# A trunk of two mixers and two FFNs: deferred conversions behind the norms, and a scan traced in two steps

## The chip, the cores and the metric

The kernel runs on one core of one Trainium2 chip. The metric is the device time of one execution in microseconds (us). A kernel has several runs, and the median is quoted.

## The reference

For one sequence of 512 tokens with 1024 features, two layers are computed. Layer 0 has a Mamba-2 (SSD) mixer, layer 1 an RG-LRU mixer; a causal ConvFFN follows each. Every part is wrapped in two RMSNorms:

```python
for i in range(DEPTH):
    h = rmsnorm(x, norm_mix_pre[i])
    m = ssd_mixer(h, ...) if i % 2 == 0 else rglru_mixer(h, ...)
    x = x + rmsnorm(m, norm_mix_post[i])
    h = rmsnorm(x, norm_ffn_pre[i])
    f = conv_ffn(h, ...)
    x = x + rmsnorm(f, norm_ffn_post[i])
```

`ssd_mixer` projects `h` to z (2048), to x, B and C (3072, through a causal convolution of 4 taps and silu) and to dt (32 heads). It scans in 4 chunks of 128 tokens for each of 4 groups of heads, gates by silu(z), norms by group, and projects by `w_out`. `rglru_mixer` projects to two branches of 1280, runs a gated linear recurrence, and projects back with a bias `b_out`. `conv_ffn` projects up to 8192, convolves with 3 taps, takes gelu(g) * v and projects down from 4096. All is float32.

## The kernel before

Four phases follow one another: the SSD mixer (`ssd`), an FFN (`ffn`), the RG-LRU mixer (`lru`), an FFN. The residual `xr` stays on chip as 4 tiles of 128 tokens x 1024 features. The input `h` of a phase is held transposed, features on partitions, as two halves `hh` (rounded to fp32r) and `hl` (the rest), so that each float32 product is made of three fp32r matmuls: `up_mm` (L227 to L229), `down_mm` (L251), `pair_mm` (L553). Each weight tile is a DMA of 512 KB on SP into `r` (class `Weight`), a rounding copy on ACT (L209) and a subtraction on DVE (L210). So ACT and DVE work in step with every 24 matmuls or so.

At the end of a phase, `down` (for the SSD mixer the loop at the end of `ssd`) holds back the last 5 (SSD: 4) weight tiles and runs them token tile by token tile, so that tile 0 is finished early. `epilogue(t)` then takes the accumulators of tile t:

- `post_norm`: squares on ACT (L190), the reciprocal root on GpSimd (L162, L163, `rstd`), the product on DVE (L193), and the residual add (L194), on GpSimd but in the last phase
- `pre_norm`: squares (ACT L169), `rstd`, product (DVE L172) into `hb`
- `transpose_h`: eight transposes on PE (L179), then `hh` on ACT (L182) and `hl` on DVE (L183)

The next phase begins with four weight tiles, which `load_ahead` loads and converts (called in the epilogue of tile 0). Their matmuls run first over tiles 0 and 1, then over tiles 2 and 3 (`HALVES`). After them come the loops over the other weights, with convolutions on ACT (L298) and DVE (L300).

The order on each engine isn't the order of the code: a scheduler of the framework places the instructions by its own simulation, and `tc.issue_after(i)` forbids it to place an instruction ahead of i. Each engine then runs its queue in order.

In `ssd`, `conv_tile` makes a projected and convolved tile. `scan_group(g)` runs the four chunks of a group: loads the decays (`cs_d`, L395), makes masked scores (L397, ACT L419 to L425, DVE), transposes (L403, L409), the weighted rows `xdt` and, on GpSimd, `xdd` (L414, which needs `dout`, made by ACT L364), then the products (L430, L432) and the state (L444). `gate(g)` projects z and norms the group by matmuls with ones and the identity (its z tiles, then a rate, then a scale). `late_consts` loads rows of constants (L144), transposes them (L147) and prepares the RG-LRU's constants after the first scan. In `lru`, `biased` adds `b_out` to each accumulator on DVE (L639) and hands the sum to the epilogue.

At the start, x tiles 0 and 1 come as two DMAs each, then the first gain as a broadcast to 128 partitions (`load_gain`, L115), and the first two `pre_norm`s.

Of the kernel before, what the change touches and what calls it, by code (L numbers as in the profile page):

```python
# [13 lines left out]
P = 128  # L14
# [6 lines left out]
NG = 4  # L21
# [54 lines left out]
def tile_trunk(ctx: ExitStack, tc: tile.TileContext, x, norm_mix_pre, norm_mix_post, norm_ffn_pre, norm_ffn_post,  # L76
# [41 lines left out]
    def load_x(t):  # L118
        for i in range(2):
            dma(xr[:, t, cols(i)], x[0, t * P:(t + 1) * P, cols(i)])  # L120

    load_x(0)
    qg = load_gain(norm_mix_pre[0])
    load_x(1)
    for i, a in enumerate((ssd_dt_bias, ssd_a_log)):
        dma(small_tiles["hrow"][i:i + 1, :], a)
    dma(small_tiles["dall"], ssd_d.to_broadcast([P, NH]))
# [4 lines left out]
    G.memset(ones, 1.0)  # L132
    stat_ids = list(range(48))
# [5 lines left out]
    def const_cols(name, parts, banks):  # L139
        n = sum(a.shape[0] for a in parts)  # L140
        rows = S2.get()
        o = 0
        for a in parts:
            dma(rows.ap[o:o + a.shape[0], 0:P], a)  # L144
            o += a.shape[0]
        pt = banks.get()
        T.transpose(pt.ap[:, 0:n], rows.ap[0:n, 0:P], ident[0:n, 0:n])  # L147
        c = small_tiles[name]
        V.tensor_copy(c, pt.ap[:, 0:n])
        rows.free()  # L150
        pt.free()
        return c
# [8 lines left out]
    def rstd(st):  # L161
        G.tensor_scalar(out=st[:, 2:3], in0=st[:, 0:1], scalar1=st[:, 1:2], scalar2=EPS, op0=ALU.add, op1=ALU.add)  # L162
        G.tensor_tensor(out=st[:, 2:3], in0=st[:, 2:3], in1=nhalf[:, 0:1], op=ALU.pow)  # L163
        return st[:, 2:3]

    def pre_norm(t, hb, qg):
        st = small()
        for i in range(2):
            A.activation(hb.ap[:, cols(i)], xr[:, t, cols(i)], AF.Square, scale=1.0 / 32, accum_out=st[:, i:i + 1])  # L169
        r = rstd(st)  # L170
        for i in range(2):
            V.scalar_tensor_tensor(out=hb.ap[:, cols(i)], in0=xr[:, t, cols(i)], scalar=r, in1=qg.ap[:, cols(i)],  # L172
                                   op0=ALU.mult, op1=ALU.mult)
# [13 lines left out]
    def post_norm(t, src, hb, pg, final):  # L187
# [3 lines left out]
        r = rstd(st)  # L191
# [62 lines left out]
    def down(w, nk, get, done, prep, epilogue, gt, last=False):  # L254
        acc = [[PS.get(), PS.get()] for t in range(NT)]
        held = []
        for k in range(nk):
# [5 lines left out]
            ops = (a, wt.wh[:, 0, :], wt.wl[:, 0, :], k == 0, k == nk - 1)  # L263
# [40 lines left out]
    def ssd(h, prep, epilogue):  # L304
# [83 lines left out]
        def scan_group(g, bT, cT):  # L388
            hs = slice(8 * g, 8 * g + 8)
            ent = None  # L390
            for c in range(NT):
# [14 lines left out]
                pt.free()  # L406
                if c < NT - 1:
# [7 lines left out]
                psy = X.get()  # L415
# [5 lines left out]
                V.tensor_tensor(out=scv, in0=scv, in1=cbm.unsqueeze(1).to_broadcast([P, 8, P]), op=ALU.mult)  # L421
                if c > 0:
# [4 lines left out]
                csb.free()  # L427
                for e in range(8):
# [13 lines left out]
                if c < NT - 1:  # L442
# [11 lines left out]
                    ent = nent  # L454
            ent.free()


        def gate(g):
            sq = None
            for m in range(4 * g, 4 * g + 4):  # L460
# [19 lines left out]
            st = small()  # L480
            V.tensor_scalar(out=st, in0=pt.ap[:, 0:NT], scalar1=1.0 / 512, scalar2=EPS, op0=ALU.mult, op1=ALU.add)
            pt.free()
            G.tensor_tensor(out=st, in0=st, in1=nhalf, op=ALU.pow)
            V.tensor_copy(sq.ap.rearrange("p (a b) -> p a b", a=NT), st.unsqueeze(2).to_broadcast([P, NT, P]))
            pt = X.get()
            for t in range(NT):
                T.matmul(pt.ap[:, t * P:(t + 1) * P], sq.ap[:, t * P:(t + 1) * P], ident, start=True, stop=True)
            sq.free()
            for m in range(4 * g, 4 * g + 4):
                ym = y_of(m)  # L490
                V.scalar_tensor_tensor(out=ym, in0=ym, scalar=consts["clru"][:, 100 + m:101 + m], in1=pt.ap, op0=ALU.mult, op1=ALU.mult)
            pt.free()

        for g in range(NG):
            bc = SG.get()
            bT, cT = bc.ap[:, 0:S], bc.ap[:, S:2 * S]
            w = wbc if g == 0 else [up_w(w_in, DI + (16 + g) * P), up_w(w_in, DI + (20 + g) * P)]
            toks = HALVES if g == 0 else [FULL]
            conv_tile(16 + g, w[0], bT, toks)
            conv_tile(20 + g, w[1], cT, toks)  # L500
            for m in range(4 * g, 4 * g + 4):
                conv_tile(m, up_w(w_in, DI + m * P), y_of(m), [FULL])
            if g > 0:
                gate(g - 1)
            scan_group(g, bT, cT)
            bc.free()
            if g == 0:
                late_consts(X)
        gate(NG - 1)
# [46 lines left out]
    def lru(h, prep, epilogue):  # L556
# [10 lines left out]
        for m in range(NL):  # L567
            if m % 4 == 0:
                n = min(4, NL - m)
                wg = Weight([w_[0, m:m + n].rearrange("h i o -> i h o") for w_ in (lru_w_gx, lru_w_ga)], n, n * 256)  # L570
            if m < 4:
                w, pt = first[m], pts[m]
            else:
                w, pt = up_w(w_in, LW + m * P), M.get()
                up_mm(pt, w, h, FULL)
            w.free()

            xb = S2.get()
            conv(xb.ap, pt.ap, 4, lambda q: clru[:, 10 * q + m:10 * q + m + 1], lcor[:, m, 3:4])
            pt.free()  # L580
            V.tensor_tensor(out=xb.ap[:, 0:3], in0=xb.ap[:, 0:3], in1=lcor[:, m, 0:3], op=ALU.add)
            xa = Act(xb.ap, LO)
            pg = [X.get(), X.get()]
            for i in range(2):
                b = 2 * (m % 4) + i
                T.matmul(pg[i].ap, wg.wh[:, b, :], xa.ah, start=True, stop=False)
                T.matmul(pg[i].ap, wg.wh[:, b, :], xa.al, start=False, stop=False)
                T.matmul(pg[i].ap, wg.wl[:, b, :], xa.ah, start=False, stop=True)
            if m % 4 == 3:
                wg.free()  # L590


            bm, thm, am = (s[m // 2].ap[:, cols(m % 2)] for s in (bt, th, at))
            A.activation(bm, pg[0].ap, AF.Sigmoid, bias=clru[:, 70 + m:71 + m])
            A.activation(am, pg[1].ap, AF.Sigmoid, bias=clru[:, 80 + m:81 + m])
            for s in pg:
                s.free()
            V.tensor_tensor(out=bm, in0=bm, in1=xb.ap, op=ALU.mult)
            V.tensor_scalar(out=am, in0=am, scalar1=0.0, scalar2=None, op0=ALU.max)
            last = A.activation(thm, am, AF.Tanh, scale=spl[:, m:m + 1])  # L600
            for s in (xb, xa):
                s.free()
# [31 lines left out]
        bo = load_gain(lru_b_out[0])  # L634

        def biased(t, acc):
            mb = row4()
            for i in range(2):
                V.tensor_tensor(out=mb.ap[:, cols(i)], in0=acc[i].ap, in1=bo.ap[:, cols(i)], op=ALU.add)  # L639
                acc[i].free()  # L640
            epilogue(t, [mb])
            if t == NT - 1:
                bo.free()

        down(w_out, NL, lambda k: th[k // 2].ap[:, cols(k % 2)], lambda k: th[k // 2].free() if k % 2 else None, prep, biased, GT)


    def ffn(i, h, prep, epilogue):
# [14 lines left out]
        for m in range(NF):  # L663
            if m < 2:
# [140 lines left out]
```

## Time and profile before

| | |
|---|---|
| runs | 1684.53, 1686.59, 1686.98 us; median 1686.59 |
| profiled execution | 1684.68 us, its span 1683.0 |
| TensorE (PE) | 1633.1 us busy, 97% |
| VectorE (DVE) | 917.7 us, 55% |
| ScalarE (ACT) | 706.1 us, 42% |
| GpSimd (POOL) | 204.4 us, 12% |
| HBM | 162.80 MB read |

The span is the part of the profiled execution that the trace covers, and 1.7 us lie around it. Busy times are sums over instructions; matmuls are pipelined, so PE is listed as busy when the next one has already begun. The granted clock is the share of TensorE's full clock that the throttle let through, 1.00 for 2.4 GHz and 0.50 for 1.2 GHz.

### The profile page before, as it was taken

How to read it: one execution, taken by the hardware profiler on the slowest of the kernel's cores; microseconds unless marked ns; L12 is line 12 of the kernel's file. 1: busy time of each engine (PE TensorE's matmuls, PEld its weight loads, DVE VectorE, ACT ScalarE, POOL GpSimd, SP SyncE). 2: the span in 40 equal slices, each digit the busy share in tenths (PEclk: the TensorE clock that was granted, in tenths of full speed). 3: DMA queues.
4: the chain of work that ended last, by engine and by line, in shares of the span. 5: the costliest groups of instructions: out<-in, count | busy, mean ns of one | idle time of the engine just before them, and what ended most of it. 6: DMA issues, size and time to landing. Idle time of an engine off the chain costs nothing. (4 is left out here: it accounts for less than half of the span.)

```text
span 1683.0 us, 19923 instructions
## 1 busy us (share of the span) xinstructions
PE 1633.1 (97%) x7905; PEld 1358.6 (81%) x7905; DVE 917.7 (55%) x1182; ACT 706.1 (42%) x1062; POOL 204.4 (12%) x199
## 2 busy tenths in 40 slices
PE   7979999998999999999999999998999999999998
PEld 6858888777888888888888888877888888888886
DVE  6878786635644444444334487956544444443432
ACT  5384655425433333333333377634433333333331
POOL 1012021114111111110000400022111111010000
PEclk9999999999999999999999999998999999999999
DMA  7353532224433322333334133433332232223321
GB/s 205 107 127 90 125 100 82 96 90 127 122 88 88 87 79 85 88 88 100 113 103 129 32 94 100 148 103 99 114 88 86 79 99 87 80 82 102 114 74 50
DMA packets 235700, 166.24 MB, mean 99 GB/s; under 512 B 6604, under 2 KB 218808, under 8 KB 235608
## 3 DMA queue, kind: packets, MB, share of 16 engines
q1 hardware_dynamic: 235608, 164.98, 33.8%
q8 instruction: 62, 1.02, 0.2%
q14 instruction: 30, 0.25, 0.0%
HBM read 162.80 MB, written 2.16 MB: 98 GB/s over the span
## 5 line engine op out<-in xcount | busy, mean ns | idle before, releaser
L210 DVE TENSOR_TENSOR w<-r,w 128x1024 fp32r<-128x1024 f32 (+1 forms) x282 | 349.3, 1245 | 552.0 <-ACT w L209 351.4
L228 PE MATMUL ps<-hl,w 128*128 128x512 f32 (+2 forms) x1632 | 614.5, 377 | 5.9 <-DVE hl L183 5.8
L227 PE MATMUL ps<-hh,w 128*128 128x512 f32 (+2 forms) x1632 | 613.8, 378 | 3.3 <-ACT hh L182 2.5
L229 PE MATMUL ps<-hh,w 128*128 128x512 f32 (+2 forms) x1632 | 613.5, 376 | 0.0
L209 ACT ACTIVATE w<-r 128x1024 fp32r<-128x1024 f32 (+1 forms) x282 | 294.1, 1051 | 384.2 <-PE ps L228 143.7
L251 PE MATMUL ps<-w,w 128*128 128x512 f32 x1776 | 404.4, 389 | 0.6 <-DVE w L241 0.6
L251 PEld LDWEIGHTS ps<-w,w 128*128 128x128 f32 x1776 | 333.0, 188 | 69.9 <-DVE w L241 1.0
L228 PEld LDWEIGHTS ps<-hl,w 128*128 128x128 f32 (+1 forms) x1632 | 309.3, 190 | 61.4 <-DVE hl L183 7.0
L227 PEld LDWEIGHTS ps<-hh,w 128*128 128x128 f32 (+1 forms) x1632 | 308.8, 190 | 59.3 <-ACT hh L182 3.7
L229 PEld LDWEIGHTS ps<-hh,w 128*128 128x128 f32 (+1 forms) x1632 | 309.2, 190 | 54.2 <-DVE w L210 0.2
L682 POOL TENSOR_TENSOR w<-t,t 128x512 f32<-128x512 f32 x48 | 61.7, 1284 | 461.7 <-DVE t L300 443.6
L300 DVE SCALAR_TENSOR_TENSOR t<-ps,cffn0a,t 128x511 f32<-128x511 f32 (+1 forms) x128 | 95.6, 747 | 18.8 <-ACT t L298 16.5
L300 DVE SCALAR_TENSOR_TENSOR t<-ps,cffn1a,t 128x511 f32<-128x511 f32 (+1 forms) x128 | 95.3, 746 | 15.9 <-ACT t L298 13.8
L553 PE MATMUL ps<-w,w 128*128 128x512 f32 x384 | 89.9, 392 | 3.6 <-DVE w L241 1.2
L298 ACT ACTIVATE t<-ps,cffn0b 128x512 f32<-128x512 f32 x64 | 49.3, 770 | 92.7 <-PE ps L229 92.7
L553 PEld LDWEIGHTS ps<-w,w 128*128 128x128 f32 x384 | 71.4, 188 | 19.9 <-DVE w L241 2.3
L298 ACT ACTIVATE t<-ps,cffn1b 128x512 f32<-128x512 f32 x64 | 49.3, 770 | 89.8 <-PE ps L229 89.8
L162 POOL TENSOR_SCALAR stats<-stats 128x1 f32<-128x1 f32 x32 | 15.2, 477 | 568.5 <-ACT v L190 370.1
L677 ACT ACTIVATE t<-t 128x512 f32<-128x512 f32 x64 | 40.5, 632 | 94.8 <-DVE t L300 94.8
L240 ACT ACTIVATE w<-w 128x512 fp32r<-128x512 f32 (+1 forms) x62 | 39.9, 648 | 51.3 <-PE ps L251 36.8
L300 DVE SCALAR_TENSOR_TENSOR t<-ps,cssd,t 128x511 f32<-128x511 f32 (+2 forms) x72 | 52.1, 736 | 3.4 <-ACT t L298 3.0
L419 ACT ACTIVATE w<-w,t 128x128 f32<-128x128 f32 x128 | 39.1, 389 | 30.3 <-DMA w<-cs_d 20.8
(177 smaller groups left out, 961.2 us busy)
## 6 DMA issues: line engine op xcount, KB each, us to landing
r<-in_ffn_w_up_dram SPq DMA_DIRECT2D x128, 512.0 KB, 4.1
r<-in_ffn_w_down_dram SPq DMA_DIRECT2D x64, 512.0 KB, 3.6
r<-in_ssd_w_in_dram SPq DMA_DIRECT2D x40, 512.0 KB, 3.9
r<-in_lru_w_in_dram SPq DMA_DIRECT2D x20, 512.0 KB, 3.7
w<-cs_d SPq DMA_DIRECT2D x16, 512.0 KB, 5.4
r<-in_ssd_w_out_dram SPq DMA_DIRECT2D x16, 512.0 KB, 3.8
r<-in_lru_w_out_dram SPq DMA_DIRECT2D x10, 512.0 KB
xr<-in_x_dram SPq DMA_DIRECT2D x8, 256.0 KB, 4.2
```

The costliest lines, as they stand in the source:

```text
L209: A.activation(self.hi.ap[:, 0:n], r, AF.Copy)
L210: (lo or V).tensor_tensor(out=self.lo.ap[:, 0:n], in0=r, in1=self.hi.f[:, 0:n], op=ALU.subtract)
L227: T.matmul(o, w.wh[:, k, :], hh[:, :, k, :], start=(k == 0), stop=False)
L228: T.matmul(o, w.wh[:, k, :], hl[:, :, k, :], start=False, stop=False)
L229: T.matmul(o, w.wl[:, k, :], hh[:, :, k, :], start=False, stop=(k == KD - 1))
L240: A.activation(self.ah, ap, AF.Copy)
L251: T.matmul(acc[h].ap, x_[:, tk], w_[:, cols(h)], start=(first and i == 0), stop=(last and i == 2))
L298: A.activation(dst, src, AF.Identity, bias=col(k) if bias is None else bias, scale=col(k - 1))
L300: V.scalar_tensor_tensor(out=dst[:, s:S], in0=src[:, 0:S - s], scalar=col(k - 1 - s), in1=dst[:, s:S], op0=ALU.mult, op1=ALU.add)
L553: T.matmul(acc.ap, a[:, tk], b[:, u, :], start=(j == 0 and u == 0 and i == 0), stop=(j == 7 and u == 1 and i == 2))
L677: A.activation(ga.ap, ga.ap, AF.Gelu_apprx_tanh)
L682: G.tensor_tensor(out=p[-1].ap[:, cols(m % 2)], in0=ga.ap, in1=va.ap, op=ALU.mult)
```

## The change

1. **Behind the norms.** The loops of `ffn` and `lru` after the first four weight tiles are placed under `behind_norms`: nothing in them may stand ahead of the last tile's `hh` and `hl`. `load_ahead` is called by a new `fetch`, ahead of the loop over the held tiles.
2. **The residual add** (L194) is on VectorE in every phase, and `pre_norm` takes its squares in one instruction of 1024.
3. **The RG-LRU's bias** starts the accumulators, as eight matmuls over two partitions (high and low part), and `biased` goes.
4. **The scan** is split: `scores(c)` and `products(c)`, and between them units of `fill`, the next group's convolution tiles and the last group's z projections. `gate` is split into `project`, `rate` and `scale`. The second accumulators of `w_out` are taken later, and the last group's rate and scale stand in its loop.
5. **Constants**: all rows are loaded early into one slot, `late_rows`; the transposes stand in the scan's `fill`.
6. **The start**: x tiles 1 to 3 come as one DMA each; the gain as one row, spread by two matmuls with a row of ones.

The core of the diff (new indentation alone is left out):

```diff
-    qg = load_gain(norm_mix_pre[0])
+    grow = row4()
+    dma(grow.ap[0:1, :], norm_mix_pre[0:1])
     load_x(1)
...
+    def const_rows(rows, parts):
         o = 0
         for a in parts:
-            dma(rows.ap[o:o + a.shape[0], 0:P], a)
+            dma(rows[o:o + a.shape[0], :], a)
...
     def pre_norm(t, hb, qg):
         st = small()
+        A.activation(hb.ap, xr[:, t, :], AF.Square, scale=1.0 / 32, accum_out=st[:, 0:1])
+        r = rstd(st, 1)
...
-            (V if final else G).tensor_tensor(out=xr[:, t, cols(i)], in0=xr[:, t, cols(i)], in1=hb.ap[:, cols(i)], op=ALU.add)
+            V.tensor_tensor(out=xr[:, t, cols(i)], in0=xr[:, t, cols(i)], in1=hb.ap[:, cols(i)], op=ALU.add)
...
-    def down(w, nk, get, done, prep, epilogue, gt, last=False):
+    def down(w, nk, get, done, prep, fetch, epilogue, gt, last=False, bias=None):
         acc = [[PS.get(), PS.get()] for t in range(NT)]
         held = []
+        if bias:
+            for t in range(NT):
+                for i in range(2):
+                    T.matmul(acc[t][i].ap, bias[0].ap[0:2, 0:P], bias[1].ap[0:2, cols(i)], start=True, stop=False)
...
                 held.append((k, wt, ops))
+        fetch()
         for t in range(NT):
...
+            n = len(fill)
+            cur = scores(0)
+            for c in range(NT):
+                for unit in fill[n * c // NT:n * (c + 1) // NT]:
+                    unit()
+                nxt = scores(c + 1) if c < NT - 1 else None
+                products(c, *cur)
+                cur = nxt
...
+            nxt = conv_units(g + 1) if g < NG - 1 else None
+            fill = list(nxt[3]) if nxt else []
+            if g == 0:
+                fill[3] = after(fill[3], lambda: late_consts(X))
+            elif g < NG - 1:
+                z, rate, scale = gates[g - 1]
+                z, u = list(z), fill
+                u[2], u[4] = after(u[2], rate), after(u[4], scale)
+                fill = [z[0], u[0], z[1], z[2], u[1], z[3], u[2], u[3], u[4], u[5]]
+            else:
+                fill = gates[g - 1][0]
+            scan_group(g, bT, cT, fill)
...
+                if i == 0 and j == 3:
+                    last_rate()
+                if i == 0 and j == 6:
+                    last_scale()
...
-        bo = load_gain(lru_b_out[0])
-
-        def biased(t, acc):
-            mb = row4()
-            for i in range(2):
-                V.tensor_tensor(out=mb.ap[:, cols(i)], in0=acc[i].ap, in1=bo.ap[:, cols(i)], op=ALU.add)
+        b2, bh, sel, one = row4(), LO.get(F32R), S2.get(), S2.get(F32R)
+        dma(b2.ap[0:2, :], lru_b_out[0].rearrange("(o d) -> o d", o=1).to_broadcast([2, D]))
+        A.activation(bh.ap[0:2, :], b2.ap[0:2, :], AF.Copy)
...
+    def behind_norms(ph):
+        order = ExitStack()
+        for i in norms_end[ph]:
+            order.enter_context(tc.issue_after(i.ins))
+        return order
...
+    qg = [PS.get(), PS.get()]
+    for i in range(2):
+        T.matmul(qg[i].ap, small_tiles["mask"][0:1, :], grow.ap[0:1, cols(i)], start=True, stop=True)
...
             if not final:
-                pre_norm(t, hb, qg)
-                transpose_h(t, hb, *nh)
+                pre_norm(t, hb, [qg.ap[:, cols(i)] for i in range(2)])
+                norms_end[ph + 1] = transpose_h(t, hb, *nh)
```

Three places in the order of the queues follow. First DVE, from the norms of tiles 1 to 3 of the SSD mixer into the first FFN (the kernel before; L210 with `w_550` and so on are weights of the FFN's loop):

```order
L172 SCALAR_TENSOR_TENSOR v_530_3404<-xr,stats,v_490_3157 128x512 x2
L183 TENSOR_TENSOR hl_231<-ps_529_3373,hh_230 128x4x128
L193 SCALAR_TENSOR_TENSOR v_533_3457<-ps_443_2877,stats,v_489_3155 128x512
L193 SCALAR_TENSOR_TENSOR v_533_3457<-ps_447_2881,stats,v_489_3155 128x512
L210 TENSOR_TENSOR w_550_3761<-r_548_3758,w_549_3760 128x1024
L210 TENSOR_TENSOR w_554_3792<-r_552_3789,w_553_3791 128x1024
L210 TENSOR_TENSOR w_561_3834<-r_559_3831,w_560_3833 128x1024
L210 TENSOR_TENSOR w_565_3865<-r_563_3862,w_564_3864 128x1024
L183 TENSOR_TENSOR hl_231<-ps_531_3419,hh_230 128x4x128
L183 TENSOR_TENSOR hl_231<-ps_532_3426,hh_230 128x4x128
```

The same place in the changed kernel, from the norm of tile 3 on:

```order
L193 SCALAR_TENSOR_TENSOR v_533_3499<-ps_439_2853,stats,v_486_3147 128x512
L193 SCALAR_TENSOR_TENSOR v_533_3499<-ps_485_3146,stats,v_486_3147 128x512
L194 TENSOR_TENSOR xr<-xr,v_533_3499 128x512 x2
L183 TENSOR_TENSOR hl_232<-ps_531_3461,hh_231 128x4x128
L183 TENSOR_TENSOR hl_232<-ps_532_3468,hh_231 128x4x128
L172 SCALAR_TENSOR_TENSOR v_533_3499<-xr,stats,v_487_3149 128x512 x2
L183 TENSOR_TENSOR hl_232<-ps_534_3513,hh_231 128x4x128
L183 TENSOR_TENSOR hl_232<-ps_535_3520,hh_231 128x4x128
L210 TENSOR_TENSOR w_547_3749<-r_545_3746,w_546_3748 128x1024
L210 TENSOR_TENSOR w_551_3780<-r_549_3777,w_550_3779 128x1024
```

All L210 of the loop have moved behind the last L183, and the residual adds (L194) have come in.

Second, PE in the first scan before: the products of the first chunk (L430), its state (L444), and the next chunk's scores follow at once:

```order
L229 MATMUL ps_165_1137<-hh_83,w_164_1134 128x512
L403 MATMUL ps_88_677<-ident,w_23_232 128x128 x2
L403 MATMUL ps_88_677<-ident,w_24_233 128x128 x2
L430 MATMUL ps_82_644<-w_83_645,t_79_637 64x128 x8
L444 MATMUL ps_84_668<-t_81_642,t_36_309 128x512
L397 MATMUL ps_98_731<-w_45_356 128x128
L409 MATMUL ps_90_684<-ident,w_45_356 128x128
```

In the changed kernel the products are L443, the state is L457, the constants' transposes L149:

```order
L443 MATMUL ps_100_736<-w_85_655,t_82_648 64x128 x7
L409 MATMUL ps_117_836<-ident,w_26_233 128x128 x2
L409 MATMUL ps_117_836<-ident,w_27_234 128x128 x2
L228 MATMUL ps_155_1069<-hl_84,w_153_1065 128x512
...
L229 MATMUL ps_170_1158<-hh_83,w_169_1155 128x512
L457 MATMUL ps_101_749<-t_84_653,t_38_306 128x512
L416 MATMUL ps_119_843<-ident,w_47_353 128x128
L457 MATMUL ps_124_883<-t_97_720,t_38_306 128x512
L149 MATMUL ps_132_927<-ident,w_2_121 128x116
```

Between products and state now stand the end of one projection (5 matmuls) and the whole of another (24).

Third, SP before, behind the first loads of the scan (L395):

```order
L395 DMA w_108_786<-cs_d 128x8x128
L205 DMA r_242_1619<-in_ssd_w_in_dram 128x8x128
L205 DMA r_248_1658<-in_ssd_w_in_dram 128x8x128
L205 DMA r_254_1697<-in_ssd_w_in_dram 128x8x128
L144 DMA t_115_833<-in_lru_conv_w_dram 40x128
L144 DMA t_115_833<-in_lru_conv_b_dram 10x128
```

In the changed kernel the rows (L142) go ahead of the scan's loads, whose first is 12 rows behind the last line here:

```order
L205 DMA r_54_468<-in_ssd_w_in_dram 128x8x128
L205 DMA r_60_507<-in_ssd_w_in_dram 128x8x128
L142 DMA w_2_121<-in_lru_conv_w_dram 40x128
L142 DMA w_2_121<-in_lru_conv_b_dram 10x128
...
L142 DMA w_2_121<-in_ffn_conv_b_dram 64x128
L205 DMA r_72_585<-in_ssd_w_in_dram 128x8x128
L205 DMA r_86_666<-in_ssd_w_in_dram 128x8x128
```

## Rows read from the trace of the kernel before

**Rows 1.** The page: busy time and share by engine; costliest groups of instructions.

```profile
PE 1633.1 (97%) x7905; PEld 1358.6 (81%) x7905; DVE 917.7 (55%) x1182; ACT 706.1 (42%) x1062; POOL 204.4 (12%) x199
...
L251 PE MATMUL ps<-w,w 128*128 128x512 f32 x1776 | 404.4, 389 | 0.6 <-DVE w L241 0.6
```

**Rows 2.** Busy time by stretch; the first line names the columns.

```profile
core 0: us, PE busy (x) PEld busy (x) DVE busy (x) ACT busy (x) POOL busy (x), PEclk, DMA share, GB/s
0.00:30.00 30.00, 19.77 (x140) 17.75 (x141) 16.44 (x27) 16.30 (x32) 6.25 (x19) 1.00 0.87 235
90.00:132.00 42.00, 32.79 (x212) 24.64 (x212) 36.44 (x62) 31.30 (x65) 6.42 (x5) 0.92 0.38 95
300.00:360.00 60.00, 56.36 (x334) 44.72 (x333) 35.83 (x53) 20.89 (x30) 11.78 (x8) 1.00 0.26 88
405.00:435.00 30.00, 21.55 (x132) 19.86 (x131) 24.31 (x26) 17.72 (x34) 16.27 (x15) 0.83 0.53 141
940.00:970.00 30.00, 29.95 (x216) 27.98 (x215) 13.95 (x20) 12.99 (x31) 11.36 (x16) 1.00 0.06 18
1130.00:1168.00 38.00, 27.73 (x173) 24.78 (x172) 24.99 (x28) 15.07 (x31) 15.05 (x16) 0.82 0.30 87
```

**Rows 3.** PE's waits (total us, times, longest), 0:30, 90:132, 405:435, 1125:1168.

```profile
PE ps L179 <- DVE v L172: 9.7, 2, 8.1
...
PE ps L147 <- DVE t L399: 2.9, 1, 2.9
PE ps L444 <- POOL t L414: 2.8, 1, 2.8
PE ps L147 <- DMA t<-in_ffn_conv_b_dram: 2.3, 1, 2.3
...
PE ps L228 <- DVE hl L183: 4.8, 1, 4.8
PE ps L179 <- DVE v L172: 2.3, 1, 2.3
PE ps L227 <- ACT hh L182: 1.4, 1, 1.4
...
PE ps L179 <- DVE w L172: 7.8, 3, 5.0
```

**Rows 4.** Timeline of DVE and POOL at the start: start, duration, engine, line, operation.

```profile
7.27 1.42 DVE L172 SCALAR_TENSOR_TENSOR v<-xr,stats,v 128x512 f32<-128x512 f32 x2 [7.27 <-DMA v<-in_norm_mix_pre_dram]
...
5.03 0.30 POOL L162 TENSOR_SCALAR stats<-stats 128x1 f32<-128x1 f32 x1 [3.24 <-ACT v L169]
5.41 0.57 POOL L163 TENSOR_TENSOR stats<-stats,nhalf 128x1 f32<-128x1 f32 x1
```

**Rows 5.** Timelines of ACT, POOL and SP in the first scan.

```profile
99.19 0.30 ACT L364 ACTIVATE t<-t 128x128 f32<-128x128 f32 x1
...
99.57 2.88 POOL L414 TENSOR_TENSOR t<-t,t 128x512 f32<-128x512 f32 x2 [72.68 <-ACT t L364]
...
106.63 0.30 SPq L144 DMA_DIRECT2D t<-in_lru_conv_w_dram  x1
```

**Rows 6.** Timeline of DVE at the first boundary and at the next.

```profile
410.92 6.36 DVE L210 TENSOR_TENSOR w<-r,w 128x1024 fp32r<-128x1024 f32 x4
...
949.43 1.23 DVE L210 TENSOR_TENSOR w<-r,w 128x1024 fp32r<-128x1024 f32 x1 [2.47 <-ACT w L209]
```

**Rows 7.** Groups by line and shape; L194 by its durations (min/median/max); L162 in 405:435.

```profile
L553 PE MATMUL ps<-w,w 128*128 128x512 f32 x384 | 89.9, 392 | 3.6 <-DVE w L241 1.2 <-ACT w L240 1.2 <-DVE v L491 1.1
...
L194 POOL TENSOR_TENSOR xr<-xr,v x16: 1281/1298/2307, 395.8 to 955.7; 128x512 f32<-128x512 f32 x16
L194 DVE TENSOR_TENSOR xr<-xr,v x8: 679/683/686, 1658.2 to 1679.2; 128x512 f32<-128x512 f32 x8
...
L162 POOL TENSOR_SCALAR stats<-stats 128x1 f32<-128x1 f32 x5 | 5.1, 1023 | 5.1 <-ACT v L169 2.8 <-ACT v L190 2.2
```

More of the change, by code (lines that the diff above doesn't have):

```diff
@@ L262, in down @@
             done(k)
-            ops = (a, wt.wh[:, 0, :], wt.wl[:, 0, :], k == 0, k == nk - 1)
+            ops = (a, wt.wh[:, 0, :], wt.wl[:, 0, :], k == 0 and not bias, k == nk - 1)
             if k < nk - gt:
@@ L480, in gate @@
[L480 to L494, printed above, removed]
+            def rate():
+                sq, r = st["sq"], small()
+                pt = X.get()
+                for t in range(NT):
+                    T.matmul(pt.ap[:, t:t + 1], sq.ap[:, t * P:(t + 1) * P], ones[:, 0:1], start=True, stop=True)
+                V.tensor_scalar(out=r, in0=pt.ap[:, 0:NT], scalar1=1.0 / 512, scalar2=EPS, op0=ALU.mult, op1=ALU.add)
+                pt.free()
+                G.tensor_tensor(out=r, in0=r, in1=nhalf, op=ALU.pow)
+                V.tensor_copy(sq.ap.rearrange("p (a b) -> p a b", a=NT), r.unsqueeze(2).to_broadcast([P, NT, P]))
@@ new lines, in scale @@
+            def scale():
+                sq = st["sq"]
+                pt = X.get()
+                for t in range(NT):
+                    T.matmul(pt.ap[:, t * P:(t + 1) * P], sq.ap[:, t * P:(t + 1) * P], ident, start=True, stop=True)
+                sq.free()
+                for m in range(4 * g, 4 * g + 4):
+                    ym = y_of(m)
+                    V.scalar_tensor_tensor(out=ym, in0=ym, scalar=consts["clru"][:, 100 + m:101 + m], in1=pt.ap, op0=ALU.mult, op1=ALU.mult)
+                pt.free()
@@ L495, in ssd, with conv_units @@
+            return [lambda m=m: project(m) for m in range(4 * g, 4 * g + 4)], rate, scale
+        def conv_units(g):
             bc = SG.get()
             bT, cT = bc.ap[:, 0:S], bc.ap[:, S:2 * S]
-            w = wbc if g == 0 else [up_w(w_in, DI + (16 + g) * P), up_w(w_in, DI + (20 + g) * P)]
             toks = HALVES if g == 0 else [FULL]
[L499 to L502, printed above, removed]
@@ L506, in ssd @@
             bc.free()
             if g == 0:
-                late_consts(X)
-        gate(NG - 1)
+                late_rows.free()
+            if nxt:
+                bc, bT, cT, _ = nxt
+        z, last_rate, last_scale = gates[NG - 1]
+        z[0]()
+        gates[NG - 2][1]()
+        z[1]()
+        gates[NG - 2][2]()
+        z[2]()
+        z[3]()
         ya = []
-        acc = [[M.get() for t in range(NT)], [X.get() for t in range(NT)]]
+        acc = [[M.get() for t in range(NT)]]
@@ L517, in ssd @@
             if i == 1:
+                acc.append([X.get() for t in range(NT)])
                 prep()
@@ L566, in lru @@
                 up_mm(pts[m], first[m], h, tok)
[L567 to L602, printed above, removed]
@@ L633, in lru, with ffn @@
         PS.give(M)
[L634 to L648 removed]
+        b2, bh, sel, one = row4(), LO.get(F32R), S2.get(), S2.get(F32R)
+        dma(b2.ap[0:2, :], lru_b_out[0].rearrange("(o d) -> o d", o=1).to_broadcast([2, D]))
+        A.activation(bh.ap[0:2, :], b2.ap[0:2, :], AF.Copy)
+        V.tensor_scalar(out=sel.ap[0:2, 0:1], in0=ident[0:2, 1:2], scalar1=-2.0, scalar2=1.0, op0=ALU.mult, op1=ALU.add)
+        A.activation(one.ap[0:2, 0:P], ident[0:2, :], AF.Identity, bias=ones[0:2, 0:1], scale=0.0)
+        V.tensor_scalar(out=b2.ap[0:2, :], in0=b2.ap[0:2, :], scalar1=ident[0:2, 1:2], scalar2=None, op0=ALU.mult)
+        V.scalar_tensor_tensor(out=bh.ap[0:2, :], in0=bh.f[0:2, :], scalar=sel.ap[0:2, 0:1], in1=b2.ap[0:2, :], op0=ALU.mult, op1=ALU.add)
+        b2.free()
+        sel.free()
+        down(w_out, NL, lambda k: th[k // 2].ap[:, cols(k % 2)], lambda k: th[k // 2].free() if k % 2 else None, prep, fetch, epilogue, GT, bias=(one, bh))
+        one.free()
+        bh.free()
+    def ffn(i, h, prep, fetch, epilogue):
         w_up, w_dn = ffn_w_up[i], ffn_w_down[i]
```

212 lines of the change are left out of this document (137 added, 75 removed).

## The prediction

> **What bounds the kernel now.** I read the page first: TensorE is busy for 97% of the span [rows 1], so the time is TensorE's work plus what it loses. A busy engine isn't one at its peak, so the second view is the table by stretch [rows 2]. There the reader is to see two losses. One is idleness: the length of a stretch less its PE busy time. The other is the clock: with two levels, 1.2 and 2.4 GHz, a mean granted clock of 0.83 over 30 us means 0.17 x 30 us of lost work. Added up:
>
> - 90 to 132 (first scan): 9.2 idle + 0.08 x 42 = 3.4 by the clock, 12.6 us.
> - 300 to 360 (end of the first mixer): 3.6 idle, clock full.
> - 405 to 435 (first mixer to first FFN): 8.5 + 5.1 = 13.6 us.
> - 940 to 970 (first FFN to second mixer): 0.05 us.
> - 1130 to 1168 (second mixer to second FFN): 10.3 + 6.8 = 17.1 us.
> - 0 to 30: 10.2 us idle, of which 9.7 are two waits for the first norms [rows 3].
>
> That is 57 us in the five that lose; of the 49.9 us that PE idles in the whole span, 41.8 lie there. Third view: who ended each wait [rows 3]. At the first scan it is a GpSimd product (L414) and constants whose rows come late by DMA or whose copies are late on DVE; at both bad boundaries it is `hl` (DVE) or the normalized row `v`/`w` (DVE L172). The fourth view, the timelines, tells why [rows 4 to 6]. The boundary from 940 to 970 does the same norms and loses nothing: it is the yardstick for the other two.
>
> **The change part by part.**
>
> Boundary into the first FFN. Before, four lo conversions (L210) ran on DVE from 410.92 for 6.36 us [rows 6], ahead of the `hl` that PE then waited 4.8 us for [rows 3]; the clock fell behind it. In the changed order every L210 of the next loop, and on ACT every L209, stands behind the last tile's `hl`. The four weights that the next phase starts with are converted ahead of the first norm, beside the held matmuls. What is late next is tile 1's norm: a tile here has 4 x 6 held matmuls behind it, 24 x 0.228 [rows 1] = 5.5 us, where the yardstick has 5 x 6, 6.8 us. Two tiles make 2.7 us less cover, of which the faster residual add gives back about 1.2 (2 x 0.62, below). I leave 3 us of the 13.6: **gain 10.6**, bounds 4 (a wait as long as the present 2.3 at L179, and a fall of the clock, stay) and 12.
>
> Boundary into the second FFN. The held tail is the yardstick's, so the loss should come near to its 0.05. The eight bias adds (L639) leave DVE, about 8 x 0.68 by the add of the same shape [rows 7], and the copy between accumulator and norm goes. Left 2 us of 17.1: **gain 15.1**, bounds 8 and 16.5. The bias comes back as eight 128x512 matmuls, 8 x 0.228 = **1.8 us**, all on TensorE's path. Their operands need one DMA and five short steps on two partitions, long before.
>
> Residual add on VectorE. In the undisturbed phase GpSimd takes 1.30 us at best for a half row, DVE 0.68 [rows 7], and it is on the chain from accumulator to `hb`: 0.62 us less per half. The eight half rows of a boundary are 8 x 0.68 = 5.5 us more on DVE; DVE ran 13.95 of 30 us in the yardstick [rows 2], so it has the room. GpSimd's adds also slowed DVE: L210 took 6.36 / 4 = 1.59 us beside them, 1.23 alone [rows 6]. I count no term beyond what the two boundaries hold. What remains on GpSimd are the two rstd steps of each norm, 0.30 and 0.57 us when DVE is quiet [rows 4]; the first averages 1.02 us in 405 to 435 [rows 7]. If they are slowed as much next to DVE's adds, the last tile's chain is 2 x 0.72 = 1.4 us longer at each boundary, 2.9 us in all, inside the bounds above.
> The Trainium skill speaks to this on both sides: its GPSIMD Engine Reference (4.1, Engine selection) sends elementwise work on a tile to VectorE, and its Key points say that GpSimd shares its SBUF interfaces with VectorE and contends with DVE instructions that have two SBUF inputs. The residual add is such an instruction, and so is L172. By that rule the small GpSimd steps wait more than before and my sum would be 1653 in place of 1650; the traces of L210 and L162 show the contention, but not yet this pairing.
>
> First scan. PE waited 2.8 us for L414, which could not start until ACT's L364, at 99.19 deep in its queue, had made `dout` [rows 5]. Then 2.9 and 2.3 us for constants [rows 3], whose first rows SP issued at 106.63 [rows 5], behind the loads of the scan. In the changed order the products stand 24 matmuls of another projection later, so the L414 wait is covered by up to 5.5 us; L364's successor still stands as deep in ACT's queue. The constants' DMAs are now ahead of all scan loads on SP, 13 small issues between weight loads; I count them at nothing, since PE waits for no weight tile in the stretches listed, and at up to 2 us of the bound below if they push one back. Left 2 us of 12.6: **gain 10.6**, bounds 5 and 12.
>
> End of the first mixer. The z projections and the last group's rate and scale move among other matmuls; the three waits there sum to 3.6 us [rows 7]. What stays are the first weight tiles of `w_out`, 1.2: **gain 2.4**, bounds 0 and 3.5.
>
> Start. The statistics were ready at 5.98, the first product waited for the gain's broadcast until 7.27 [rows 4]. A row of 4 KB takes its place; it is also 512 KB less ahead of x tile 1, whose norm sets the first up projection. Against it, tile 1 comes as one DMA, and its second halves stand behind two gain matmuls, which run while PE has nothing else. **Gain 2**, bounds -1 and 3.5.
>
> New waits. The scans 1 to 3 are now mixed with convolutions and z projections; each chunk's products may wait for ACT, which ran 31 of 42 us in the stretch of the first scan [rows 2]. **Cost 2.5**, bounds 0 and 8. The tail is untouched.
>
> Sum: 10.6 + 15.1 - 1.8 + 10.6 + 2.4 + 2 - 2.5 = 36.4 us. The profiled execution took 1684.7, so 1648.3; the median of the runs is 1.9 above it: **1650**. All low bounds together leave a gain of 6, all high ones 46.
>
> **Rivals.**
>
> A, the norms still come late. DVE now carries adds, norms and `hl` in one queue, and one gap brings the clock down again: a single wait of 5.0 us at L179 [rows 3] went with a mean clock of 0.82. If half of the losses at the two boundaries and the first scan stays (21.6 of 43.3 in place of my 7), the gain is 14.6 us less: 1665. For it: tile 1 has less cover in the first boundary, and nothing shortens the two rstd steps. Against: 0.05 us lost in the yardstick with slower adds.
>
> B, slower: the scans starve TensorE. A convolution's PSUM bank comes free by ACT's first pass, which may now stand behind a chunk's exponentials. If each of the 12 chunks of the scans 1 to 3 cost what the first product did in the first scan, 2.8 us [rows 3], and as much again by half a clock for some 3 us, that is 12 x 4.3 = 52 us against the gains of 38.9: 1684.7 + 13 + 1.9, about 1700. It decides from 3.2 us per chunk on. Against: such waits do not show in the scans before, where ACT has the same work in one piece.
>
> C, the conversions put behind the norms only move the wait: the next loop's third weight comes late. The first four tiles are 4 x 24 x 0.228 = 21.9 us of cover, and four L210 take 4.9 from about 14 us on, so it needs a backlog of several us more. All given back would be 1687, the median of before.
>
> **How the numbers follow.** Forecast 0.69 (1638 to 1661), A 0.19 (1661 to 1674), B 0.08, C 0.04. The range of 8 in 10 takes the forecast's own and most of A: 1634 to 1672. A measurement of this kernel tells 0.2%, 3.4 us, from no change: faster 0.88 (forecast and A), same 0.04 (C), slower 0.08 (B).
>
> **What would show it.** Right: the stretches of both boundaries with PE busy to within 3 us and a granted clock of 1.00 (or one dip); no wait of PE for L147's successor or for the state product above 1 us; the first L172 before 6.5 us, against 7.27 now. A: waits at L179 for DVE's L172 of 2 us or more with a clock below 0.9. B: PE's busy share in 130 to 300 below 95%. C: PE waits for `w` from L210 some 25 us into an FFN. The forecast is wrong if the sum of idle and clock loss in the five stretches stays above 35 us.

## The result and the profile after

The change takes 1655.35 us (median of 4 runs, 1654.79 to 1659.9) against 1686.78 before in the same session: ratio 0.9823, 95% interval 0.9811 to 0.9834; 31 us less by the medians, 30 by the ratio. The forecast was 1650, in a range of 1634 to 1672. The profiled execution took 1655.42 us, its span 1653.7.

The same events in both kernels tell where the 29.3 us between the two profiled executions lie. The rows are matmuls of the transposes (L179) at the start and at the three boundaries, then of the two projections down (L251): durations, then first and last start. Before:

```profile
L179 PE MATMUL ps<-ident,v x32: 272/347/476, 8.1 to 22.7; 128*128 128x128 f32 x32
L179 PE MATMUL ps<-ident,v x32: 270/272/446, 405.0 to 430.1; 128*128 128x128 f32 x32
L179 PE MATMUL ps<-ident,v x32: 270/272/273, 941.1 to 963.0; 128*128 128x128 f32 x32
L251 PE MATMUL ps<-w,w x240: 388/389/497, 1076.6 to 1132.6; 128*128 128x512 f32 x120
L179 PE MATMUL ps<-ident,w x32: 272/273/448, 1124.9 to 1162.9; 128*128 128x128 f32 x32
L251 PE MATMUL ps<-w,w x768: 388/389/389, 1501.3 to 1675.1; 128*128 128x512 f32 x192
```

After:

```profile
L179 PE MATMUL ps<-ident,v x32: 270/273/476, 8.5 to 21.1; 128*128 128x128 f32 x32
L179 PE MATMUL ps<-ident,v x32: 270/272/273, 390.9 to 411.5; 128*128 128x128 f32 x32
L179 PE MATMUL ps<-ident,v x32: 270/272/273, 916.2 to 937.7; 128*128 128x128 f32 x32
L251 PE MATMUL ps<-w,w x240: 387/389/795, 1061.0 to 1120.5; 128*128 128x512 f32 x120
L179 PE MATMUL ps<-ident,v x32: 270/272/273, 1110.6 to 1132.1; 128*128 128x128 f32 x32
L251 PE MATMUL ps<-w,w x768: 388/389/389, 1472.0 to 1645.8; 128*128 128x512 f32 x192
```

Read as running gains: 1.6 us by the end of the start (22.7 against 21.1), 14.1 by the end of the first mixer (405.0 against 390.9), 24.9 at the second mixer's entry (941.1 against 916.2), but only 15.6 at its projection down and 14.3 at the first transposes behind it (1124.9 against 1110.6): **10.6 us are given back inside the second mixer**. Then 29.3 by the last FFN's projection, and the same at the end.

The stretches of [rows 2] now, each placed by these events (same columns):

```profile
0.00:30.00 30.00, 23.29 (x150) 18.89 (x151) 16.73 (x28) 15.91 (x25) 5.03 (x19) 1.00 0.85 227
90.00:132.00 42.00, 41.97 (x270) 33.09 (x269) 38.56 (x87) 28.04 (x55) 7.86 (x6) 1.00 0.42 117
292.00:352.00 60.00, 60.00 (x278) 49.93 (x277) 27.00 (x30) 18.11 (x20) 4.89 (x4) 1.00 0.31 97
388.00:418.00 30.00, 28.72 (x208) 26.61 (x207) 21.37 (x31) 14.64 (x27) 4.92 (x10) 1.00 0.07 20
1035.00:1075.00 40.00, 34.21 (x130) 26.72 (x129) 31.98 (x37) 18.07 (x26) 0.00 (x0) 0.87 0.34 111
1106.00:1136.00 30.00, 30.00 (x203) 27.53 (x202) 20.12 (x30) 13.90 (x29) 5.20 (x12) 1.00 0.00 1
```

The first scan lost 12.6 us by idle time and clock and now loses nothing; both boundaries, 13.6 and 17.1, lose 1.3 and nothing, at full clock. The new loss is the stretch from 1035 to 1075: 5.8 us idle and 0.13 x 40 = 5.2 by the clock. That sum counts a little twice, since the clock falls before the wait is over. Cut finer:

```profile
1055.00:1060.00 5.00, 2.25 (x5) 1.79 (x6) 5.00 (x7) 2.74 (x4) 0.00 (x0) 0.67 0.43 116
1060.00:1065.00 5.00, 5.00 (x12) 3.46 (x11) 5.00 (x7) 0.07 (x1) 0.00 (x0) 0.50 0.70 227
1065.00:1070.00 5.00, 5.00 (x18) 3.62 (x17) 0.16 (x1) 0.00 (x0) 0.00 (x0) 0.80 0.53 185
```

A mean of 0.67 over 5 us is 3.3 us at half clock; with the next two lines it is 3.3 + 5 + 2 = 10.3 us, and PE works in 2.2 + 5 + 2 = 9.2 of them. Half of that, 4.6 us, is lost, so 10.4 us with the wait. PE's longest waits (total, times, longest) say whose it is:

```profile
PE ps L260 <- DVE w L712: 5.8, 1, 5.8
PE ps L815 <- DMA v<-in_norm_mix_pre_dram: 4.1, 1, 4.1
PE ps L227 <- DVE hl L183: 2.1, 3, 1.1
```

L260 are the bias matmuls, L712 is the last step that makes their operand. DVE's timeline shows it in the queue:

```profile
1050.35 0.72 DVE L711 TENSOR_SCALAR v<-v,ident 2x1024 f32<-2x1024 f32 x1
...
1052.80 1.21 DVE L210 TENSOR_TENSOR w<-r,w 128x1024 fp32r<-128x1024 f32 x1
1053.93 1.27 DVE L700 TENSOR_TENSOR w<-w,t 128x512 f32<-128x512 f32 x2
1055.13 1.28 DVE L241 TENSOR_TENSOR w<-w,w 128x512 fp32r<-128x512 f32 x2
1056.34 1.27 DVE L712 SCALAR_TENSOR_TENSOR w<-w,t,v 2x1024 fp32r<-2x1024 f32 x1
```

DVE runs without a pause there, behind the recurrence's scans; between L711 and L712 stand eight other instructions, while PE, done with the mixer's projections at 1052, needs the result of L712 first of all and gets it at 1057.6.

### The profile page after: what moved, and what is told of

The parts are those of the page before. It is cut to its first block, busy times and chain, and to the rows that moved or that the text cites. A ratio compares the mean times of both kernels' runs of the same rounds, so it can differ in the third digit from the quotient of the medians.

```text
span 1653.7 us, 19927 instructions
## 1 busy us (share of the span) xinstructions
PE 1630.6 (99%) x7917; PEld 1355.3 (82%) x7917; DVE 922.8 (56%) x1201; ACT 704.0 (43%) x1032; POOL 162.3 (10%) x175
## 4 chain that ended last, share of the span: by engine, by line
PE 96%; DVE 2%; DMA 1%; ACT 1%; POOL 0%; issue 0%; SPq 0%; POOLq 0%; DVEq 0%; ACTq 0%
PE ps L251 25%; PE ps L227 20%; PE ps L229 20%; PE ps L228 20%; PE ps L623 5%; PE ps L443 1%; DMA w<-cs_d 1%; PE ps L179 1%; PE ps L445 1%; PE ps L457 1%; DVE w L210 0%; PE ps L409 0%; DMA xr<-in_x_dram 0%; ACT w L425 0%; PE ps L657 0%
## 5 line engine op out<-in xcount | busy, mean ns | idle before, releaser
L210 DVE TENSOR_TENSOR w<-r,w 128x1024 fp32r<-128x1024 f32 (+1 forms) x282 | 347.1, 1238 | 552.1 <-ACT w L209 333.6
L209 ACT ACTIVATE w<-r 128x1024 fp32r<-128x1024 f32 (+1 forms) x282 | 294.2, 1051 | 382.0 <-PE ps L228 149.5
L251 PE MATMUL ps<-w,w 128*128 128x512 f32 x1776 | 407.9, 391 | 0.0
L251 PEld LDWEIGHTS ps<-w,w 128*128 128x128 f32 x1776 | 334.8, 189 | 70.4 <-issue 0.9
L227 PEld LDWEIGHTS ps<-hh,w 128*128 128x128 f32 (+1 forms) x1632 | 305.1, 188 | 59.0 <-DVE hl L183 2.8
L229 PEld LDWEIGHTS ps<-hh,w 128*128 128x128 f32 (+1 forms) x1632 | 305.9, 187 | 54.8 <-issue 0.9
L305 DVE SCALAR_TENSOR_TENSOR t<-ps,cffn1a,t 128x511 f32<-128x511 f32 (+1 forms) x128 | 95.3, 746 | 16.1 <-ACT t L303 14.1
L162 POOL TENSOR_SCALAR stats<-stats 128x1 f32<-128x1 f32 x32 | 10.0, 311 | 608.8 <-ACT v L190 550.2
```

Source lines behind the costliest of these rows:

```text
L209: A.activation(self.hi.ap[:, 0:n], r, AF.Copy)
L210: (lo or V).tensor_tensor(out=self.lo.ap[:, 0:n], in0=r, in1=self.hi.f[:, 0:n], op=ALU.subtract)
L227: T.matmul(o, w.wh[:, k, :], hh[:, :, k, :], start=(k == 0), stop=False)
L229: T.matmul(o, w.wl[:, k, :], hh[:, :, k, :], start=False, stop=(k == KD - 1))
L251: T.matmul(acc[h].ap, x_[:, tk], w_[:, cols(h)], start=(first and i == 0), stop=(last and i == 2))
L305: V.scalar_tensor_tensor(out=dst[:, s:S], in0=src[:, 0:S - s], scalar=col(k - 1 - s), in1=dst[:, s:S], op0=ALU.mult, op1=ALU.add)
```

## The experiments

Each run is set against the kernel before in its own session; the change's ratio is 0.9823 (0.9811 to 0.9834).

**The bias matmuls moved** to the head of each tile's held tail.

```diff
-        if bias:
-            for t in range(NT):
...
         for t in range(NT):
+            if bias:
+                for i in range(2):
+                    T.matmul(acc[t][i].ap, bias[0].ap[0:2, 0:P], bias[1].ap[0:2, cols(i)], start=False, stop=False)
```

> The eight bias matmuls of the RG-LRU's output stand at the head of the held tail of each token tile instead of ahead of the first w_out matmul. Theory 1 (their operand, DVE L712, comes late and nothing else is late there): the 5.8 us wait and the clock's fall behind it go, some 10.9 us by the trace, so about 1644.5 us. Rival (DVE as a whole is behind at that place, so the first w_out weights or activations are as late): PE waits for L210 or L241 instead, 2 to 5 us stay with a fall of the clock, 1649 to 1654 us.

1648.0 us, ratio 0.9777 (0.9762 to 0.9793). The stretch holds:

```profile
1035.00:1075.00 40.00, 38.54 (x169) 31.23 (x168) 36.98 (x43) 22.10 (x31) 0.00 (x0) 1.00 0.39 123
```

1.5 us idle and a full clock, against 10.4 us lost. The wait and the clock behind it are gone, and the run is shorter by 6.9 us by the spans (1646.8 against 1653.7), 7.3 by the medians. That is less than the 10.9 of theory 1: 0.5 was counted twice, 1.5 stays as small waits (1.3 of them is the rival's, PE waits for an activation of the down projection), and for some 2 us no wait accounts.

**The wait kept, PE kept busy in it**, by 26 matmuls whose result is overwritten.

```diff
+            for n in range(26):
+                T.matmul(acc[0][0].ap, fill[:, 0, 0, 0:P], fill[:, :, n % KD, :], start=True, stop=True)
             for t in range(NT):
                 for i in range(2):
                     T.matmul(acc[t][i].ap, bias[0].ap[0:2, 0:P], bias[1].ap[0:2, cols(i)], start=True, stop=False)
```

> 26 matmuls of 128x512 with operands that are long there, whose result is overwritten, stand ahead of the bias matmuls: 26 x 0.227 = 5.9 us of work in a wait of 5.8 us. The wait for the operand stays. Theory 1 (about 5 us of the 10.9 lost there are TensorE's clock at 1.2 GHz after the idle time, and a busy engine keeps it): no fall of the clock there, about 1650.5 us. Rival (the loss is the wait alone, and the slow stretch has another cause): 1655 us, the clock falls there as before.

1653.1 us, 0.981 (0.9792 to 0.9827): 2.4 us less by the spans (1651.3 against 1653.7), half of what theory 1 said, and not clear of nothing by the intervals. The trace is clearer: the clock is at half for 3.4 us (a mean of 0.66 over 5 us) in place of 10.3, but it doesn't hold quite:

```profile
1055.00:1060.00 5.00, 5.00 (x23) 3.77 (x22) 5.00 (x7) 2.78 (x6) 0.00 (x0) 1.00 0.31 105
1060.00:1065.00 5.00, 5.00 (x16) 3.77 (x15) 5.00 (x8) 0.85 (x1) 0.00 (x0) 0.66 0.63 211
```

PE is busy all the time and yet the clock falls for a part of 1060 to 1065, right behind the eight bias matmuls, whose operands have 2 of 128 partitions (2.1 us of such). With these in pairs among full matmuls (the bias moved) it didn't fall. That the bias matmuls let it fall is likely but not shown: no run has the 26 others without them.

**The bias added on DVE again** (`biased` and `load_gain` as before, no bias matmuls).

> The changed kernel with the RG-LRU's output bias added on DVE again, ahead of each norm, and no bias matmuls. Theory 1 (the wait for the bias operand and the clock behind it cost 9 to 11 us, the eight matmuls 1.8, and eight adds of 0.68 us are covered by the held tail): 1642 to 1646 us. Rival (the adds load the boundary as they did before): 4 to 8 us come back at the second mixer's boundary, 1647 to 1651 us.

1652.7 us, 0.9798 (0.9784 to 0.9813): between the bias moved and the change, and above both expected ranges. The rival holds in kind: the adds come back at the boundary, with PE's waits

```profile
PE ps L179 <- DVE w L172: 4.8, 3, 2.0
```

and, from 1096 to 1136, 5.4 us idle in all and 0.96 of the clock. So the matmuls are the better way, put late, by some 5 us; put first, they cost 1 to 4 us more than the adds, by spans, medians or ratios, which is at the edge of what the intervals tell.

**The residual add on GpSimd again**, all else as changed.

```diff
-            V.tensor_tensor(out=xr[:, t, cols(i)], ...
+            (V if final else G).tensor_tensor(out=xr[:, t, cols(i)], ...
```

> The changed kernel with the residual add on GpSimd again, the order behind the norms kept: no L210 between the norms. Theory 1 (conversions were the loss; the slower add of 1.30 against 0.68 us per half row lengthens each tile's chain by about 1.2 us, which the held matmuls cover but at the first boundary): 1 to 4 us more, 1656 to 1659 us. Rival (GpSimd's slow add and its contention were the loss): 10 us or more, over 1665 us.

1661.0 us, 0.9853 (0.9838 to 0.9869): 5 to 7 us more, above theory 1's range and below the rival's. At the first boundary PE waits 1.2 us for `hl` and 0.8 for the norm, and the clock falls again (a mean of 0.96 from 385 to 430, against 1.00).

**No order behind the norms.**

```diff
-        for i in norms_end[ph]:
-            order.enter_context(tc.issue_after(i.ins))
         return order
```

> The changed kernel without the order behind the norms; the weights ahead are fetched before the held tiles and the residual add is on VectorE, as in the change. The order that comes out has no L210 between the norms. Theory 1 (what counts is that no conversion stands between the norms, by whatever means): the same as the change, 1655 us within 3. Rival (the order behind the norms does something of its own, as for the convolutions): a fall of the clock at a boundary is back, 1661 us or more.

1671.3 us, 0.9908 (0.9893 to 0.9923): 14 to 16 us more. The premise of the expectation was wrong. DVE's timeline at the first boundary has eight L210 between the norms, here the first four:

```profile
397.02 1.21 DVE L210 TENSOR_TENSOR w<-r,w 128x1024 fp32r<-128x1024 f32 x1
398.15 0.68 DVE L194 TENSOR_TENSOR xr<-xr,v 128x512 f32<-128x512 f32 x1
398.75 1.22 DVE L210 TENSOR_TENSOR w<-r,w 128x1024 fp32r<-128x1024 f32 x1
399.89 0.68 DVE L194 TENSOR_TENSOR xr<-xr,v 128x512 f32<-128x512 f32 x1
400.49 2.35 DVE L210 TENSOR_TENSOR w<-r,w 128x1024 fp32r<-128x1024 f32 x2
402.76 1.28 DVE L183 TENSOR_TENSOR hl<-ps,hh 128x512 fp32r<-128x512 f32 x2
```

PE waits for the `hl` behind them (385 to 425):

```profile
PE ps L228 <- DVE hl L183: 4.2, 1, 4.2
PE ps L227 <- DVE hl L183: 1.7, 1, 1.7
```

At both boundaries a fall of the clock is back (0.96 and 0.91 over 40 us), the sign that the rival named. So the run doesn't tell "no conversion between the norms" from "the order" by itself; that it is the conversions is read from the trace, where ACT's (L209) stand ahead of `hh` as DVE's do ahead of `hl`. What is shown is that the explicit order keeps them out, and the early fetch and the faster add don't.

**Neither the order nor the early fetch; then neither the order nor the add on VectorE.**

> The changed kernel without the order behind the norms and with the weights ahead fetched in the first tile's epilogue again; the residual add stays on VectorE. The order has 8 L210 between the norms at both mixer boundaries. Theory 1 (the conversions are the loss): 15 to 25 us more than the change, 1670 to 1680 us. Rival (the residual add on VectorE is what helps): 1655 to 1660 us.

> The changed kernel without the order behind the norms and with the residual add on GpSimd again; the weights ahead are still fetched before the held tiles. The order puts 8 L210 between the norms at both mixer boundaries again. Theory 1 (the conversions among the norms are the loss): the first boundary loses 8 to 12 us more, the second 8 to 16 more, 1672 to 1683 us. Rival (the slow residual add is the loss): the same as the run with the residual add on GpSimd alone.

1672.6 us, 0.9917 (0.9903 to 0.9932), and 1675.8 us, 0.9942 (0.9926 to 0.9958). Without the order, the early fetch is worth about 1 us, which the intervals don't tell from nothing, and the faster add some 5. Both lie in theory 1's ranges: with the conversions among the norms most of the boundaries' loss is back, whichever engine adds. Three parts were not undone by themselves: the early fetch with the order kept, the squares in one instruction, and the start.

**The scan.** Four variants: the fill ahead of a one-step scan; the fill behind it, as before; constants' rows late; the last two together.

```diff
-                nxt = scores(c + 1) if c < NT - 1 else None
-                products(c, *cur)
+                products(c, *scores(c))
...
+            rows = S2.get()
+            const_rows(rows.ap[:, 0:P], parts)
+            c = const_cols(name, rows.ap[:, 0:P], banks)
```

> The changed kernel with the fill units traced ahead of the scan and each chunk's scores and products in one step; constants stay early. Theory 1 (of the 12.6 us lost in the first scan, 5.2 were waits for constants and some of the clock's 3.4 went with them; the rest, the wait for the state product, was the one-step scan): the first scan loses 3 to 6 us, the others little, 1658 to 1662 us. Rival 1 (the scheduler mixes the projections in by itself, the two steps do nothing): 1655 us. Rival 2 (the one-step scan was the loss): 1667 us or more.

> The changed kernel with each chunk's scores and products in one step and the fill units traced behind the whole scan, as the kernel before had the next group's projections; constants early, their transposes behind the first scan. Theory 1 (the order of tracing decides how far the scheduler spreads the scan; the wait for the state product, 2.8 us, comes back in the first scan, with a fall of the clock): 1660 to 1664 us. Rival (as with the fill ahead of the scan, 1657.5, the scheduler mixes by itself): 1655 to 1658 us.

> The changed kernel with the constants' rows loaded late again, into short-lived slots, just ahead of their transposes; the two-step scan stays, and the transposes stand in its fill. Theory 1 (rows that SP issues behind the scan's loads make PE wait, 2 to 3 us for each of two transposes, and the clock falls): the first scan loses 5 to 9 us more, 1660 to 1664 us. Rival (with projections between the chunks the transposes find their rows anyway): 1655 us within 2.

> Both undone: one-step scan with the fill behind it, and constants' rows late. Theory 1 (the two causes add up to the first scan's 12.6 us): 1665 to 1670 us, with a clock below 0.95 in the first scan. Rival (the first scan's loss came mostly from one of them): the same as the worse of the two single runs.

| variant | us | ratio (95%) |
|---|---|---|
| fill ahead, one step | 1657.5 | 0.9829 (0.9813 to 0.9845) |
| fill behind, one step | 1666.7 | 0.9882 (0.9867 to 0.9897) |
| rows late, two steps | 1658.6 | 0.9832 (0.9817 to 0.9847) |
| fill behind, one step, rows late | 1661.6 | 0.9852 (0.9836 to 0.9868) |

The split in two steps alone does little (1 to 2 us, inside the intervals), the scheduler mixes by itself when the projections stand ahead (rival 1 there). Traced behind the scan, they cost 10 to 11 us, more than either reading expected. The first scan then loses 6.5 us idle with a clock of 0.92 over its 42 us; PE's waits are for constants' copies, conversions and convolutions, not the state product that theory 1 named:

```profile
PE ps L416 <- DVE cffn1a L150: 1.9, 1, 1.9
PE ps L229 <- DVE w L210: 1.9, 2, 1.2
PE ps L227 <- DVE t L305: 1.3, 1, 1.3
```

Late rows cost 1.5 us by the ratios and 3 by the medians, which the intervals don't tell from nothing; that is less than theory 1, and no wait for a row is left. Together the two cost 5 to 6 us, less than the fill behind alone: they don't add, and both readings of the last expectation fell. In that run the first scan loses only 1.8 us, at full clock, and PE idles 5.1 us in the scans behind it (132 to 300). Each variant is a new schedule, and which small wait comes out last isn't told by the part that was undone. How much of the 12.6 us belongs to which part stays open.

**Both kernels beaten?** The bias moved, ACT's table loaded early, and two conversions put behind the first norms.

```diff
+    A.activation(small()[:, 3:4], ones[:, 0:1], AF.Square)
...
-    ssd_first.append(up_w(ssd_w_in[0], DI + 16 * P))
...
             if t == 0:
+                ssd_first += [up_w(ssd_w_in[0], DI + i * P) for i in (16, 20)]
```

> The run with the bias matmuls at the head of the held tails, and at the start a small activation that loads ACT's table before x lands, and the first two convolution weights converted behind the first norms. Theory (the table load stood 1.3 us behind x tile 0 on ACT, and a conversion of 1.2 us ahead of the first hl on DVE): the first up projection starts 1.5 to 2.5 us earlier than at 13.1 to 13.8 us, 1645 to 1647 us, faster than both kernels. Rival (x tile 1 by its DMA sets the start): no change to the run with the bias moved alone, 1648 us.

1649.0 us, 0.9771 (0.9758 to 0.9785). Faster than both kernels, but not than the bias moved alone (0.9777): the edits of the start gain nothing. ACT's timeline has the reason, the rival's:

```profile
0.79 1.28 ACT L138 ACT_TABLE_LOAD   x1 [0.79 <-PEq L891]
...
4.28 1.06 ACT L171 ACTIVATE v<-xr 128x1024 f32<-128x1024 f32 x1 [2.00 <-DMA xr<-in_x_dram]
...
7.11 1.06 ACT L171 ACTIVATE v<-xr 128x1024 f32<-128x1024 f32 x1 [1.68 <-DMA xr<-in_x_dram]
```

Tile 0's squares start at 4.28 now, in place of 5.54, but tile 1's wait for its DMA until 7.11, and the first up projection needs both tiles. It starts at 13.18, where the run with the bias moved alone has 13.07.

## Why the prediction was right, and where it was not

By the events above, the forecast's terms come out so (us gained):

| part | forecast | by the events |
|---|---|---|
| start | 2 | 1.6 |
| first mixer: scan, end, new waits | 10.6 + 2.4 - 2.5 = 10.5 | 14.1 - 1.6 = 12.5 |
| first boundary and FFN | 10.6 | 24.9 - 14.1 = 10.8 |
| second mixer: the bias matmuls | -1.8 | 14.3 - 24.9 = -10.6 |
| second boundary and FFN | 15.1 | 29.3 - 14.3 = 15.0 |
| sum | 36.4 | 29.3 |

- **Boundaries.** Right in kind, and 10.8 and 15.0 against 10.6 and 15.1. That the sizes fit so well is in part luck: less was left than I allowed (1.3 and nothing, for 3 and 2), and less had been lost than I counted. My sums of idle time and clock count the time twice in which PE idles at the low clock. At the second boundary that was much, as from 1136 to 1142 of the kernel before:

```profile
1136.00:1142.00 6.00, 2.73 (x10) 2.07 (x10) 5.09 (x6) 3.68 (x7) 0.00 (x0) 0.50 0.74 210
```

  Of 13.7 us at half clock there PE worked 9.2, so 14.9 us were lost, not 17.1; at the first boundary 12.3, not 13.6. The runs show the order behind the norms as the main cause, 14 to 16 us for both, the faster add with 5 to 7 more, and the bias adds that left the second one (5.4 us idle with them back). Rival A fell: PE's waits for L172 are 1.2 us in all.
- **The residual add.** I counted no term of its own for it; it has one, 5 to 7 us. The small GpSimd step L162 that I feared for is in the groups by line of the first boundary, from 385 to 435 before (first line) and in the run without the order (second), from 385 to 415 after (third):

```profile
L162 POOL TENSOR_SCALAR stats<-stats 128x1 f32<-128x1 f32 x8 | 6.6, 822 | 53.3 <-ACT v L190 49.5 <-ACT v L169 3.6
...
L162 POOL TENSOR_SCALAR stats<-stats 128x1 f32<-128x1 f32 x7 | 4.6, 664 | 22.0 <-ACT v L169 15.5 <-ACT v L190 6.4
...
L162 POOL TENSOR_SCALAR stats<-stats 128x1 f32<-128x1 f32 x7 | 2.9, 413 | 18.3 <-ACT v L169 16.7 <-ACT v L190 1.4
```

  That is 0.82 us before, 0.66 with the conversions and DVE's adds, 0.41 with the adds alone: the conversions slowed the step, the adds hardly do. At the second boundary it took 0.3 us both before and after. The Trainium skill's contention rule (GPSIMD Engine Reference, Key points) shows in [rows 6, 7], but the 2.9 us that I made of it were not due. The Trainium skill's advice there (4.1, Engine selection) held: the add took 0.68 us on DVE, 1.36 on GpSimd in the run that gave it back.
- **The bias.** This is the step that failed: "Their operands need one DMA and five short steps on two partitions, long before." The eight matmuls were priced at 1.8 us and their place at nothing; by the events the mixer gave back 8.8 more, with 5.8 of waiting and 4.6 by the clock in the trace. The steps are short, but the last of them stood in DVE's queue behind eight other instructions until 1056.34; that queue wasn't looked at. With the bias moved, the span is 36.2 us below the one before (1646.8 against 1683.0), the 36.4 that was forecast.
- **First scan, end of the mixer.** Gains of 10.6 and 2.4 forecast; no idle time is left in either stretch, and the new waits are 1.8 us of the 2.5 (PE busy 166.2 of 168 us from 132 to 300). One of them is the state product's (L457 behind DVE's L507), 1.2 us, where none was to be above 1. That the two steps are what brings the gain was wrong: tracing the projections ahead of or among the scan does.
- **Start.** 1.6 us of the 2, but not by the way named: the first L172 starts at 7.69, later than 7.27 [rows 4] and than the 6.5 that was to show it, since ACT's table load stood behind x (at 4.24, 0.78 before). What was gained is mostly the clock: the first up projection begins no earlier, but its matmuls, 0.42 us long at half clock before (first line), begin at full.

```profile
13.52 0.42 PE L227 MATMUL ps<-hh,w 128*32 128x256 f32 x1
...
13.78 0.30 PE L227 MATMUL ps<-hh,w 128*32 128x256 f32 x1 [1.08 <-DVE hl L183]
13.92 0.28 PE L228 MATMUL ps<-hl,w 128*32 128x256 f32 x1
```

  PE ran the gain's four matmuls from 4.14 on, where its first work was at 8.08 before. That these bring the clock isn't shown: in the last run they stand there too, and the projection's first five matmuls are still at half clock.
- **Sum.** 36.4 forecast, 29.3 between the profiled executions: 8.8 less by the bias's place, and 2 more from the first mixer. The second is luck, since the two steps that I named aren't what brought it.

## What to carry to other kernels

On an engine that runs in order, a conversion that is free in the middle of a phase is dear between a norm and the transposes behind it: say so to the scheduler, and move it behind. A new operand for the first matmul of a stage is priced by the queue of the engine that makes it, not by its own microseconds; let the matmul that needs it come late in the accumulation. After a large gain, look for the place that gave some back: here one edit moved gains another 7 us.

## What the runs showed that I had not expected

Behind 2.1 us of matmuls on 2 of 128 partitions the granted clock fell to a mean of 0.66 over 5 us although PE never paused; that they were the reason is likely, not shown. Nor does the length of one pause tell: with the add on GpSimd the clock fell behind waits of 0.8 and 1.2 us close together, and with the bias moved it held through one of 1.3. A schedule isn't additive: the fill behind a one-step scan and late rows together cost 5 to 6 us, the fill behind it alone 10 to 11.
